# Group 1 of three feed-forward blocks by seven products instead of eight

## The chip, the cores and the metric

The kernel runs on one core of one Trainium2 chip. The metric is device time of one execution in microseconds; the number before the change is the median of three runs, 929.22 us (928.6 to 930.41).

The core's engines that matter: PE (matrix multiply, into eight PSUM banks), DVE (elementwise work), ACT (copies, casts, activation functions), POOL and SP (which here mainly issue transfers from memory). Each engine has its own queue of instructions.

## What is computed

A two-layer encoder trunk on 256 tokens with 1024 channels, in float32. Each layer is

```
x = x + 1/2 * SwiGLU_1(RMSNorm(x))
h = RMSNorm(x);  [qA kA vA qB kB vB] = h @ W_in
x = x + concat(windowed attention A, differential attention B) @ W_out
x = x + 1/2 * SwiGLU_2(RMSNorm(x))
```

with a last RMSNorm, and `swiglu(h) = (silu(h @ w_gate) * (h @ w_up)) @ w_down`. `w_gate` and `w_up` are 1024 x 2816, `w_down` 2816 x 1024. So there are four feed-forward blocks (FFNs), and in this document they are numbered in the order in which they run: 1 and 2 in the first layer, 3 and 4 in the second. The attention parts are not touched by the change.

## The kernel before

**Precision.** Every float32 product is made of three matmuls. An operand is split in a high part (a cast to float32r) and a low part (value minus high part); the product is high·high + low·high + high·low. For the weights the split is done in the kernel: for each half of a weight step, ACT casts (`act.copy(h_, r_)`) and DVE subtracts (`dve.tensor_tensor(l_, r_, f(h_), op=ALU.subtract)`), in `emit_split`. In the profile these are the groups `w<-raw` on ACT and `w<-raw,w` on DVE, 128x1024 each.

**Weight steps.** The list `specs` holds all weight blocks in the order in which PE uses them. A step in an FFN is a block of four 128-row chunks by 512 columns (1 MB). `weights()` takes the next step and calls `ahead(n)`, which writes down loads (`emit_dma`, queue SP), preparations and splits up to half-step n. `look[0]` says how many half-steps the splits run ahead of PE's use: with step i about to be used, half-steps up to 2i + look are written down, and one more when PE reaches the second half of the step (`Split.part`). `IN_FFN` is 8, `IN_MIX` 6.

**Raw buffers.** A loaded block lives in a buffer with the tag `raw`, six of them. The dictionary `raws` keeps the blocks that are still needed; a further load is written down only while it has fewer than `N_RAW = 6` entries. The first two blocks of the kernel are loaded and split by generators (`early`); their entries are removed at the very end of a generator, after its last `yield`.

**An FFN** works on five groups of 512 columns of gate and up (0 to 4), a last part of 256 columns, and the down projection, which runs one group behind. Group 0 needs x as it becomes ready; the inverse norms `r` come from `norm.stats()`, which ends in a small power instruction on POOL. SiLU (ACT) uses r as its scale; the elementwise product `up()` (DVE, two instructions called "ups" below) makes the hidden block h. At the next group PE transposes h (`turn`: four transposes for each of two halves into PSUM, then an ACT cast and a DVE subtraction), and the down projection uses the result. A plain group has 96 matmuls for gate and up and 48 for down.

**Seven products.** Groups in `SEVEN = (2, 3, 4)` do gate and up as a 2 by 2 block product (two token tiles by two halves of the 1024 channels, times two halves of the channels by gate and up) with seven block products of 12 matmuls, `by_seven`. Its weight steps, made by `seven()`, come from four blocks: a (gate, channels 0 to 511), b (up, same), c (up, channels 512 to 1023), d (gate, same). The steps are a; b + c (`bc`); d; c; down0; a + b; that + c; that + d; down1. The sum b + c and the sum a + b are made by transfers from memory on POOL's queue that accumulate into a raw block (`gather`); c and d are added by DVE (`plus`, the group `raw<-raw,raw`). The other side needs four sums of x, made once per FFN by `make_sums()` from float32 copies (`copies()`, eight ACT instructions): each is a DVE subtraction or addition, an ACT cast and a DVE subtraction for its low part. They are made inside group 1, which is plain. The products are combined by seven DVE additions and subtractions (`put`) and two ACT copies.

**Order.** Each engine's instructions keep the order in which the program writes them (`Kept`, `tc.keep_in_program_order`), except inside attention. So the place of a call in the Python text sets what stands behind what on DVE, ACT and POOL. This is the plain group 1 before, with the sums between its parts:

```
tokens(gs, norm.xs, weights(), 0); hT = turn(h, 2); norm.copies()
tokens(gs, norm.xs, weights(), 4); g = gate(gs); next(sums, None)
for k0 in (0, 4): tokens(us, norm.xs, weights(), k0); next(sums, None)
h = hidden(g, us)
for hh in range(2): down(hT, n - 1, hh, weights()); ...
```

Of the kernel before, what the change touches and what calls it, by code (L numbers as in the profile page):

```python
# [12 lines left out]
ALU = mybir.AluOpType  # L13

P = 128
D = 1024
S = 256
# [10 lines left out]
AHEAD = 10  # L28
N_RAW, N_S4 = 6, 28
IN_FFN, IN_MIX = 8, 6  # L30
SEVEN = (2, 3, 4)


@with_exitstack
def trunk(ctx: ExitStack, tc: tile.TileContext, x, n1, g1, u1, d1, nm, w_in, sink,
# [4 lines left out]
    class Kept:  # L40


        def __init__(self, eng):
            self.eng = eng
# [67 lines left out]
        kn = src.shape[1]  # L112
        return Step(kn, n, lambda t: [(t, src)], **how)

    def seven(wg, wu, c0, downs):
# [21 lines left out]
        return [Step(4, 512, load(a), key=a, free=[]),  # L137
                Step(4, 512, load(b), key=b, behind=gather(c, b), prep=gather(b, a)),
                Step(4, 512, load(d), key=d, free=[]),
                Step(4, 512, load(c), key=c, free=[]),  # L140
                downs[0],
                Step(4, 512, None, src=a, free=[]),
                Step(4, 512, None, prep=plus(c, a), src=a, free=[c]),
                Step(4, 512, None, prep=plus(d, a), src=a, free=[a, d]),
                downs[1]]

    def emit_dma(i):
        s = specs[i]
        raws[s.key] = raw = wp.tile([P, s.kn, s.n], F32, tag="raw", bufs=N_RAW, name=nm_("raw"))
        for dst, src in s.moves(raw):  # L150
            if i > 1:
                sp.dma_start(dst, src)
            else:
                for k in range(s.kn):
                    sp.dma_start(dst[:, k:k + 1], src[:, k:k + 1])
                    yield
        if s.behind is not None:
            s.behind()

    class Split:  # L160

# [79 lines left out]
        return w  # L241

    for l in range(DEPTH):
        def ffn_specs(wg, wu, wd):
            down = lambda g, h: plain(wd[l], h * 512, 512, 4 * g, 4)
            for k0 in (0, 4):
                specs.extend(plain(w[l], 0, 512, k0, 4) for w in (wg, wu))
            for g in range(1, NGRP):
                downs = [down(g - 1, h) for h in range(2)]
                if g in SEVEN:  # L250
                    specs.extend(seven(wg[l], wu[l], g * 512, downs))
# [11 lines left out]
        ffn_specs(g1, u1, d1)  # L263
# [21 lines left out]
        ffn_specs(g2, u2, d2)  # L285


    xk = const.tile([P, 2, D], F32, name="xk")

    class Norm:  # L290


        def __init__(self, g0, sums=len(SEVEN) > 0):
# [39 lines left out]
        def make_sums(self):  # L333

            self.sm = []

            (t0, t1), (b0, b1) = [(t[:, :, 0:P], t[:, :, P:S]) for t in self.xg]

            def make(x, y, op):
                v = tmp().rearrange("p a (c s) -> p (a c) s", c=2)  # L340
                dve.tensor_tensor(v, x, y, op=op)
                tag, n = ("q", 3) if len(self.sm) < 3 else ("v", 1)
                sm = tp.tile([P, 2, 512], F32R, tag=tag, bufs=n, name=nm_(tag)).rearrange("p a (c s) -> p (a c) s", c=2)
                act.copy(sm[:, :, 0:P], v)
                dve.tensor_tensor(sm[:, :, P:S], v, f(sm[:, :, 0:P]), op=ALU.subtract)
                self.sm.append(sm)
                return v

            s1 = make(b1, t1, ALU.subtract)
# [18 lines left out]
        def stats(self, n=512):  # L368
# [41 lines left out]
    def take_x(k):  # L410
# [8 lines left out]
        elif k == 1:  # L419
# [6 lines left out]
            norm.pair(3)  # L426
            norm.squares(0, 512, 512)
        elif k == 2:
            ahead(7)
            norm.squares(1, 512, 512)  # L430
            norm.stats()
            constants()
# [131 lines left out]
            elif k == 2:  # L564
                self.nxt.stats()

    def ffn(norm, aside=None, before=None, final=False):
        def silu(out_, acc, t):
            act.activation(out_, acc, AF.Silu, scale=norm.r[:, t:t + 1])
            return out_  # L570
# [25 lines left out]
                pe.matmul(acc, lhsT=xh, rhs=lo, start=False, stop=k == 3)  # L596
            return acc

        def by_seven(h, g):


            flat = lambda: tmp().rearrange("p a n -> p (a n)")
# [3 lines left out]
                return o  # L606

            m1, m7 = flat(), flat()
            act.copy(m1, prod(norm.quarter(0, 0), weights()))
            act.copy(m7, prod(norm.summed(2), weights(held=True)))  # L610
            hT = turn(h, 2)
            p2 = prod(norm.quarter(0, 1), weights())
            g0 = put(flat(), p2, m1, ALU.add)
            p3 = prod(norm.summed(3), weights())
            silu(g0, g0, 0)
            down(hT, g - 1, 0, weights())
            h = blk(F32)
            p5 = prod(norm.summed(0), weights())
            late = g == max(SEVEN)
# [14 lines left out]

        def turn(hs, n):
            out_ = []
            for i in range(n):
                sl = halves(bank())
                for c in range(2):
                    for t in range(2):  # L640
# [12 lines left out]
        gs, us = [bank(), bank()], [bank(), bank()]  # L653
        if before is None:
            before = norm.late
        look[0] = IN_FFN
        before(0)
        ws = (weights(), weights(2))
        for k in (0, 2):
# [2 lines left out]
            for sl, w in zip((gs, us), ws):  # L662
                tokens(sl, norm.xs, w, 0, (k, k + 1))
        before(2)
        tokens(gs, norm.xs, weights(), 4)
        g = gate(gs)
        tokens(us, norm.xs, weights(), 4)
        h = hidden(g, us)
        for n in range(1, NGRP):
            sums = norm.make_sums() if n + 1 == min(SEVEN, default=0) else iter(())  # L670
            if n in SEVEN:
                look[0] = IN_FFN - max(0, n - 2) if before is not take_x else IN_MIX - (n == NGRP - 1)
                h = by_seven(h, n)
                continue
            gs = [bank(), bank()]
            tokens(gs, norm.xs, weights(), 0)
            hT = turn(h, 2)
# [30 lines left out]
    def ffn_end(parts, last):  # L708
# [39 lines left out]
    def mix(l, norm, nxt_norm):  # L748
# [215 lines left out]
        def out_part(w, k0, h, order=None):  # L964
            tokens(accs[h], oT, w, k0, range(2), order=order, h=h)

        for k0 in (0, 2, 4):
            w = weights()
            for h in range(2):
# [25 lines left out]

    for l in range(DEPTH):
        final = l == DEPTH - 1
        parts = ffn(norm, attention_constants, take_x) if l == 0 else ffn(norm)
        norm_m = Norm(16 + l * 8, False)
        ffn_close(parts, norm_m)  # L1000
        norm2 = Norm(32 + l * 8)
# [80 lines left out]
```

## Time and profile before

| | |
|---|---|
| median of three runs | 929.22 us |
| profiled execution, its time | 928.39 us |
| profiled execution, its span | 926.6 us |
| PE busy | 915.1 us |
| DVE busy | 760.8 us |
| ACT busy | 568.7 us |
| bytes read from memory | 192.71 MB |

The profiled execution is 0.8 us below the median, and its span, from the first to the last instruction, 1.8 us below its own time. In the profile nearly every instruction has line L50, that of the wrapper `Kept`, so groups are told apart by what they write and read: `ps<-w,s` is a matmul of x or h with weights, `ps<-w,q` and `ps<-w,v` one with a sum of x, `ps<-ident,s` a transpose of h, `tmp<-ps,tmp` a combination of products. A row of the timeline has start, length, engine, operation, tiles and count; in brackets behind it stands how long the engine was idle before it and what it waited for. A row with a count covers several instructions in a run. [...] FFN 1 runs from 5 to about 188 us, FFN 2 from about 286 to 472, FFN 3 from about 463 to 645, FFN 4 from about 741 to the end.

### The profile page before, as it was taken

How to read it: one execution, taken by the hardware profiler on the slowest of the kernel's cores; microseconds unless marked ns; L12 is line 12 of the kernel's file. 1: busy time of each engine (PE TensorE's matmuls, PEld its weight loads, DVE VectorE, ACT ScalarE, POOL GpSimd, SP SyncE). 2: the span in 40 equal slices, each digit the busy share in tenths (PEclk: the TensorE clock that was granted, in tenths of full speed). 3: DMA queues.
4: the chain of work that ended last, by engine and by line, in shares of the span. 5: the costliest groups of instructions: out<-in, count | busy, mean ns of one | idle time of the engine just before them, and what ended most of it. 6: DMA issues, size and time to landing. Idle time of an engine off the chain costs nothing.

```text
span 926.6 us, 12551 instructions
## 1 busy us (share of the span) xinstructions
PE 915.1 (99%) x4732; PEld 771.7 (83%) x4732; DVE 760.8 (82%) x1074; ACT 568.7 (61%) x893; POOL 59.5 (6%) x77
## 2 busy tenths in 40 slices
PE   8999999999999999999999999999999999999997
PEld 6888887899888888888888888888998888888886
DVE  6759999969876579999776799996698676799994
ACT  7836675557755557576475466565578475566561
POOL 0500000000000001000000000000001000001011
PEclk9999999999999999999999999999999999999999
DMA  9986897827434859797767597887462377597731
GB/s 338 358 224 195 253 279 262 239 98 222 135 124 167 255 152 264 188 261 270 260 234 194 144 298 204 252 279 204 114 226 92 137 231 197 143 292 221 229 118 46
DMA packets 110893, 194.58 MB, mean 210 GB/s; under 512 B 3566, under 2 KB 31280, under 8 KB 110832
## 3 DMA queue, kind: packets, MB, share of 16 engines
q1 hardware_dynamic: 96528, 166.74, 53.1%
q0 software_dynamic: 12928, 25.46, 15.4%
q10 hardware_dynamic: 1376, 1.57, 0.5%
q8 instruction: 37, 0.61, 0.3%
q14 instruction: 24, 0.20, 0.1%
HBM read 192.71 MB, written 1.05 MB: 209 GB/s over the span
## 4 chain that ended last, share of the span: by engine, by line
PE 84%; DVE 9%; issue 2%; DMA 2%; ACT 1%; POOLq 0%; ACTq 0%; POOL 0%; DVEq 0%
PE ps L50 84%; DVE w L50 6%; DMA raw<-in_ffn_w_up_dram 2%; DVE tmp L50 2%; DVE raw L50 1%; ACT w L50 1%; DVE s L50 1%; DMA xk<-in_x_dram 0%; ACT s L50 0%; DVE xk L50 0%; POOLq L1077 0%; ACTq L50 0%; ACT tmp L50 0%; POOL rf L50 0%; DVEq L50 0%
## 5 line engine op out<-in xcount | busy, mean ns | idle before, releaser
L50 PE MATMUL ps<-w,s 128*128 128x512 f32 (+1 forms) x2754 | 640.9, 391 | 0.5 <-DVE w L50 0.5
L50 PEld LDWEIGHTS ps<-w,s 128*128 128x128 f32 x2754 | 512.1, 188 | 106.5 <-DVE w L50 1.2
L50 DVE TENSOR_TENSOR w<-raw,w 128x1024 fp32r<-128x1024 f32 (+1 forms) x440 | 461.1, 1095 | 58.8 <-ACT w L50 57.8
L50 ACT CAST w<-raw 128x1024 fp32r<-128x1024 f32 (+1 forms) x440 | 390.8, 948 | 90.6 <-DVE raw L50 68.1
L50 PE MATMUL ps<-w,q 128*128 128x512 f32 x432 | 101.9, 389 | 0.0
L50 PEld LDWEIGHTS ps<-w,q 128*128 128x128 f32 x432 | 81.1, 188 | 16.8
L50 PE MATMUL ps<-s,w 128*128 128x256 f32 x672 | 84.0, 285 | 0.0
L50 PEld LDWEIGHTS ps<-s,w 128*128 128x128 f32 x672 | 81.7, 192 | 1.1
L50 ACT ACTIVATE s<-ps,gcol 128x256 fp32r<-128x256 f32 (+1 forms) x80 | 31.4, 488 | 44.6 <-PE ps L50 42.9
L50 DVE TENSOR_TENSOR raw<-raw,raw 128x1024 f32<-128x1024 f32 x48 | 56.5, 1218 | 0.0
L50 POOL DMA_DIRECT2D raw<-in_ffn_w_up_dram x24 | 31.1, 1295 | 352.5 <-DVE w L50 166.5
L50 ACT CAST s<-ps 128x512 fp32r<-128x512 f32 x44 | 23.9, 592 | 40.7 <-PE ps L50 40.7
L50 DVE TENSOR_TENSOR s<-ps,s 128x512 fp32r<-128x512 f32 x44 | 28.4, 683 | 19.9 <-ACT s L50 19.9
L50 PE MATMUL ps<-ident,s 128*128 128x128 f32 x304 | 40.5, 274 | 0.6 <-DVE s L50 0.6
L50 PEld LDWEIGHTS ps<-ident,s 128*128 128x128 f32 x304 | 35.0, 140 | 6.9 <-DVE s L50 1.5
L50 ACT ACTIVATE tmp<-tmp,r 128x512 f32<-128x512 f32 x24 | 17.3, 722 | 33.8 <-DVE tmp L50 33.8
L50 ACT ACTIVATE s<-s,negm 128x256 f32<-128x256 f32 x64 | 31.9, 501 | 6.6 <-DVE negm L50 6.4
L50 PE MATMUL ps<-w,v 128*128 128x512 f32 x144 | 34.6, 389 | 0.0
L50 ACT CAST q<-tmp 128x512 fp32r<-128x512 f32 x20 | 12.4, 621 | 35.0 <-DVE tmp L50 34.9
L50 PEld LDWEIGHTS ps<-w,v 128*128 128x128 f32 x144 | 27.0, 188 | 5.6
L50 DVE SCALAR_TENSOR_TENSOR s<-ps,gcol,s 128x256 fp32r<-128x256 f32 x48 | 20.3, 478 | 12.1 <-ACT s L50 12.0
L50 ACT COPY tmp<-ps 128x512 f32<-128x512 f32 x28 | 16.3, 583 | 22.5 <-PE ps L50 22.0
(106 smaller groups left out, 419.5 us busy)
## 6 DMA issues: line engine op xcount, KB each, us to landing
raw<-in_ffn_w_down_dram SPq DMA_DIRECT2D x44, 1024.0 KB, 5.5
raw<-in_ffn_w_gate_dram SPq DMA_DIRECT2D x39, 1024.0 KB, 5.6
raw<-in_ffn_w_up_dram SPq DMA_DIRECT2D x39, 1024.0 KB, 5.3
raw<-in_ffn_w_up_dram POOLq DMA_DIRECT2D x24, 1024.0 KB, 10.4
raw<-in_w_in_dram SPq DMA_DIRECT2D x14, 1024.0 KB, 5.4
raw<-in_ffn_w_gate_dram SPq DMA_DIRECT2D x8, 512.0 KB, 6.4
raw<-in_ffn_w_up_dram SPq DMA_DIRECT2D x8, 512.0 KB, 7.4
raw<-in_w_in_dram SPq DMA_DIRECT2D x8, 512.0 KB, 5.3
```

Of the source, the lines that this page charges most:

```text
L50: ins = issue(*a, **k)
```

## The change

- FFNs 2, 3 and 4 do groups 1 to 4 by seven products; FFN 1 keeps groups 2 to 4.
- In group 1 the steps come in another order: a; d; down0; c; b + c; a + b; + c; + d; down1. So two products with unsummed x and weights and the first half of the down projection stand in front of the products with sums.
- The float32 copies of x and the first two sums move into group 0, the other two into group 1 between its products; the low part of a sum is made one call later than the sum (`low`), and the order of the last two sums is exchanged.
- h is transposed in two halves, one behind each of the first two products.
- In group 0 the splits run 7 half-steps ahead in place of 8; from group 1 to 4 it is 8, 7, 6, 5 (before: 8, 7, 6 from group 2 to 4).
- Accumulating transfers that would be written down while POOL still has to make the next r are kept in a list (`issue`, `hold`) and written right behind it (`flush`).
- The generators of the first two blocks are run to their end, so that their two entries leave `raws`: six blocks instead of four can then be entered. The number of buffers stays six.

```diff
-SEVEN = (2, 3, 4)
+SEVEN = ((2, 3, 4), (1, 2, 3, 4))
...
+        bc = Step(4, 512, load(b), key=b, behind=gather(c, b))
+        rest = [Step(4, 512, load(d), key=d, free=[]), Step(4, 512, load(c), key=c, free=[]), downs[0]]
+        steps = [rest[0], rest[2], rest[1], bc] if first else [bc] + rest
+        steps[0].prep = lambda: issue(gather(b, a))
+        return [Step(4, 512, load(a), key=a, free=[])] + steps + [
                 Step(4, 512, None, src=a, free=[]),
                 Step(4, 512, None, prep=plus(c, a), src=a, free=[c]),
                 Step(4, 512, None, prep=plus(d, a), src=a, free=[a, d]),
...
+    def issue(add):
+        pending.append(add)
+        if not hold[0]:
+            flush()
+
+    def flush():
+        hold[0] = False
+        while pending:
+            pending.pop(0)()
...
             s1 = make(b1, t1, ALU.subtract)
+            s2 = make(s1, t0, ALU.add)
+            low(0, s1)
             yield
-            s2 = make(s1, t0, ALU.add)
+            b0_ = make(b0, s2, ALU.subtract)
+            low(1, s2)
             yield
-            make(t1, t0, ALU.subtract)
+            v = make(t1, t0, ALU.subtract)
+            low(2, b0_)
             yield
-            make(b0, s2, ALU.subtract)
+            low(3, v)
             yield
...
             pool.tensor_tensor(self.r, ms, mhalf[:, 0:2], op=ALU.pow)
+            flush()
...
         elif k == 2:
+            for e in early:
+                next(e, None)
             ahead(7)
...
+                w = weights()
+                next(sums, None)
+                p1 = prod(norm.quarter(0, 0), w)
+                hT = turn(h, (0,))
+                w = weights()
+                next(sums, None)
+                act.copy(m1, p1)
+                p2 = prod(norm.quarter(0, 1), w)
+                hT += turn(h, (1,))
+                w = weights()
+                next(sums, None)
+                g0 = put(flat(), p2, m1, ALU.add)
+                silu(g0, g0, 0)
+                down(hT, 0, 0, w)
+                p3 = prod(norm.summed(2), weights())
+                act.copy(m7, prod(norm.summed(3), weights()))
...
-        look[0] = IN_FFN
+        look[0] = IN_FFN - (1 in sevens)
...
-        tokens(gs, norm.xs, weights(), 4)
+        w = weights()
+        sums = iter(())
+        if 1 in sevens:
+            norm.copies()
+            sums = norm.make_sums()
+        tokens(gs, norm.xs, w, 4)
         g = gate(gs)
-        tokens(us, norm.xs, weights(), 4)
+        w = weights()
+        next(sums, None)
+        tokens(us, norm.xs, w, 4)
         h = hidden(g, us)
...
-                look[0] = IN_FFN - max(0, n - 2) if before is not take_x else IN_MIX - (n == NGRP - 1)
-                h = by_seven(h, n)
+                look[0] = IN_FFN + min(sevens) - n if before is not take_x else IN_MIX - (n == NGRP - 1)
+                h = by_seven(h, n, sums)
...
         look[0] = IN_MIX
+        hold[0] = True
```

More of the change, by code (lines that the diff above doesn't have):

```diff
@@ L113, in plain, with seven @@
         return Step(kn, n, lambda t: [(t, src)], **how)
-    def seven(wg, wu, c0, downs):
+    def seven(wg, wu, c0, downs, first):
         a, b, c, d = [object() for _ in range(4)]
@@ L135, in plus @@
             return prep
[L137 to L141, printed above, removed]
+        bc = Step(4, 512, load(b), key=b, behind=gather(c, b))
[3 more added lines that the diff above has]
+        return [Step(4, 512, load(a), key=a, free=[])] + steps + [
                 Step(4, 512, None, src=a, free=[]),
@@ L157, in emit_dma @@
         if s.behind is not None:
-            s.behind()
+            issue(s.behind)
+    pending, hold = [], [False]
+    def issue(add):
[6 more added lines that the diff above has]
+            pending.pop(0)()
     class Split:
@@ L249, in ffn_specs @@
                 downs = [down(g - 1, h) for h in range(2)]
-                if g in SEVEN:
-                    specs.extend(seven(wg[l], wu[l], g * 512, downs))
+                if g in sevens:
+                    specs.extend(seven(wg[l], wu[l], g * 512, downs, g == 1))
                 else:
@@ L284, in trunk, with __init__ @@
         fine.update(range(mixed + 2, len(specs)))
-        ffn_specs(g2, u2, d2)
+        ffn_specs(g2, u2, d2, SEVEN[1])
     xk = const.tile([P, 2, D], F32, name="xk")
     class Norm:
-        def __init__(self, g0, sums=len(SEVEN) > 0):
+        def __init__(self, g0, sums=True):
             self.g0, self.xs, self.sums = g0, [], sums
@@ L565, in late, with ffn @@
                 self.nxt.stats()
-    def ffn(norm, aside=None, before=None, final=False):
+    def ffn(norm, aside=None, before=None, final=False, sevens=SEVEN[1]):
         def silu(out_, acc, t):
@@ L597, in prod, with by_seven @@
             return acc
-        def by_seven(h, g):
+        def by_seven(h, g, sums):
             flat = lambda: tmp().rearrange("p a n -> p (a n)")
@@ L608, in by_seven @@
             m1, m7 = flat(), flat()
[L609 to L616, printed above, removed]
+            if g > 1:
+                act.copy(m1, prod(norm.quarter(0, 0), weights()))
+                act.copy(m7, prod(norm.summed(3), weights(held=True)))
+                hT = turn(h, 2)
+                p2 = prod(norm.quarter(0, 1), weights())
+                g0 = put(flat(), p2, m1, ALU.add)
+                p3 = prod(norm.summed(2), weights())
+                silu(g0, g0, 0)
+                down(hT, g - 1, 0, weights())
+            else:
+                w = weights()
[9 more added lines that the diff above has]
+                next(sums, None)
+                g0 = put(flat(), p2, m1, ALU.add)
+                silu(g0, g0, 0)
+                down(hT, 0, 0, w)
+                p3 = prod(norm.summed(2), weights())
+                act.copy(m7, prod(norm.summed(3), weights()))
             h = blk(F32)
             p5 = prod(norm.summed(0), weights())
-            late = g == max(SEVEN)
+            late = g == max(sevens)
             p6 = prod(norm.summed(1), weights(look[0] - 5 if late else 0, late))
@@ L636, in turn @@
             out_ = []
-            for i in range(n):
+            for i in (range(n) if isinstance(n, int) else n):
                 sl = halves(bank())
@@ L965, in out_part @@
             tokens(accs[h], oT, w, k0, range(2), order=order, h=h)
+        hold[0] = True
         for k0 in (0, 2, 4):
@@ L997, in trunk @@
         final = l == DEPTH - 1
-        parts = ffn(norm, attention_constants, take_x) if l == 0 else ffn(norm)
+        parts = ffn(norm, attention_constants, take_x, sevens=SEVEN[0]) if l == 0 else ffn(norm)
         norm_m = Norm(16 + l * 8, False)
```

11 lines of the change are left out of this document (6 added, 5 removed).

## The prediction

> **What bounds the kernel now.** I read the page first, then the chain of waits, then the stages of one feed-forward block (FFN), and last its instructions in order of time.
>
> ```profile
> span 926.6 us, 12551 instructions
> PE 915.1 (99%) x4732; PEld 771.7 (83%) x4732; DVE 760.8 (82%) x1074; ACT 568.7 (61%) x893; POOL 59.5 (6%) x77
> PE 84%; DVE 9%; issue 2%; DMA 2%; ACT 1%; POOLq 0%; ACTq 0%; POOL 0%; DVEq 0%
> ...
> 132.63 0.98 PE L50 MATMUL ps<-ident,s 128*128 128x128 f32 x7 [0.34 <-DVE s L50]
> 150.97 13.46 PE L50 MATMUL ps<-w,s 128*128 128x512 f32 x58 [0.54 <-DVE w L50]
> ```
>
> PE works 915.1 of 926.6 us, so a matmul that goes away can shorten the run. But the chain runs through DVE for 9% without PE standing still there: DVE arrives just in time, and in the first FFN twice too late (0.34 and 0.54 us). Which engine would arrive last after the change is read from the stages of the second FFN: group 0's last part, group 1 (plain), groups 2, 3 and 4 (seven products).
>
> ```profile
> 293.40:315.29 21.89, 21.89 (x100) 18.08 (x99) 13.78 (x18) 13.84 (x20) 2.03 (x2) 1.00 0.84 246
> 315.29:346.13 30.84, 30.84 (x142) 25.66 (x141) 21.77 (x24) 19.04 (x28) 1.28 (x1) 1.00 0.57 167
> 346.13:376.94 30.81, 30.81 (x142) 25.61 (x140) 27.76 (x29) 20.02 (x23) 2.57 (x2) 1.00 0.94 263
> 376.94:407.79 30.85, 30.85 (x142) 25.61 (x141) 30.27 (x32) 19.82 (x23) 2.57 (x2) 1.00 0.80 230
> 407.79:437.60 29.81, 29.81 (x137) 24.79 (x136) 29.67 (x33) 19.30 (x24) 0.00 (x0) 1.00 0.79 253
> ```
>
> The columns are length, then busy time of PE, weight loads, DVE, ACT, POOL, then granted clock, DMA share and GB/s. PE is full in all. DVE is idle 8.1 us in group 0's part and 9.1 in group 1, 3.1 in group 2, and 0.6 and 0.1 in groups 3 and 4: groups of seven live on a lead that DVE has won in groups 0 and 1. The change takes group 1's slack.
>
> **The gain.** A plain group has 2 tensors x 2 token tiles x 8 chunks x 3 matmuls = 96 for gate and up, seven products 7 x 4 x 3 = 84: 12 fewer, beside 48 of the down projection.
>
> ```profile
> 293.42 22.03 PE L50 MATMUL ps<-w,s 128*128 128x512 f32 x96
> 315.29 1.04 PE L50 MATMUL ps<-ident,s 128*128 128x128 f32 x8
> 348.85 1.03 PE L50 MATMUL ps<-ident,s 128*128 128x128 f32 x8
> 349.64 2.98 PE L50 MATMUL ps<-w,s 128*128 128x512 f32 x12
> 360.62 5.60 PE L50 MATMUL ps<-w,q 128*128 128x512 f32 x24
> 366.06 11.04 PE L50 MATMUL ps<-w,s 128*128 128x512 f32 x48
> ```
>
> 24 matmuls start 5.44 us before the next row (360.62 to 366.06): 0.227 each; eight transposes take 0.79 (348.85 to 349.64). Twelve are 2.72 us, in three FFNs 8.2 us. With nothing else the profiled 928.39 becomes 920.2.
>
> **What is added.** Each FFN gets six more half-step splits (an ACT cast and a DVE subtraction each), four DVE additions of raw blocks, seven DVE additions of products, two ACT copies and two accumulating transfers on POOL; the sums of x (four additions, casts and subtractions) stay eight DVE instructions but move to an earlier time.
>
> ```profile
> 303.96 1.28 ACT L50 ACT_TABLE_LOAD   x1 [3.02 <-PE ps L50]
> 305.26 1.27 ACT L50 ACTIVATE tmp<-ps,r 128x512 f32<-128x512 f32 x2
> 306.42 3.89 ACT L50 CAST w<-raw 128x1024 fp32r<-128x1024 f32 x4
> 307.50 2.36 DVE L50 TENSOR_TENSOR w<-raw,w 128x1024 fp32r<-128x1024 f32 x2 [3.31 <-ACT w L50]
> 309.77 1.40 DVE L50 SCALAR_TENSOR_TENSOR s<-ps,hr,tmp 128x512 f32<-128x512 f32 x2
> 315.92 1.07 ACT L50 CAST s<-ps 128x512 fp32r<-128x512 f32 x2 [5.62 <-PE ps L50]
> 316.54 1.29 DVE L50 TENSOR_TENSOR s<-ps,s 128x512 fp32r<-128x512 f32 x2 [3.10 <-ACT s L50]
> 316.88 3.04 ACT L50 ACTIVATE s<-ps,gcol 128x256 f32<-128x256 f32 x8
> 320.90 2.36 DVE L50 TENSOR_TENSOR w<-raw,w 128x1024 fp32r<-128x1024 f32 x2 [3.07 <-ACT w L50]
> 323.17 0.68 DVE L50 TENSOR_TENSOR tmp<-s,s 128x512 f32<-128x512 f32 x1
> 323.89 0.62 ACT L50 CAST q<-tmp 128x512 fp32r<-128x512 f32 x1 [0.92 <-DVE tmp L50]
> 324.55 0.69 DVE L50 TENSOR_TENSOR q<-tmp,q 128x512 fp32r<-128x512 f32 x1 [0.69 <-ACT q L50]
> 346.38 0.59 ACT L50 COPY tmp<-ps 128x512 f32<-128x512 f32 x1 [3.29 <-PE ps L50]
> 352.73 2.35 DVE L50 TENSOR_TENSOR raw<-raw,raw 128x1024 f32<-128x1024 f32 x2
> 360.22 9.16 DVE L50 TENSOR_TENSOR w<-raw,w 128x1024 fp32r<-128x1024 f32 x8
> 361.39 8.63 ACT L50 CAST w<-raw 128x1024 fp32r<-128x1024 f32 x9
> 374.63 2.00 DVE L50 TENSOR_TENSOR tmp<-tmp,ps 128x512 f32<-128x512 f32 x3
> ```
>
> Spacings: a split 1.15 us on DVE (9.16/8), a cast 0.96 on ACT (8.63/9), a raw addition 1.15 (2.35/2, following ones closer), a product addition 0.65, a sum, its cast and its low part 0.62 to 0.69 with 0.04 of handover (323.17, 323.89, 324.55), the two products with SiLU ("ups") 1.40. DVE gets 6.9 + 4.6 + 4.6 = 16.1 us more per FFN. Before, the five windows left it 21.0 idle; after them 21.0 - 16.1 - 2.7 = 2.2 would remain, so there is room only if DVE never waits.
>
> It does wait, since engines keep the written order. The row at 320.90 shows it: DVE stood 3.07 us for a cast, although the sum behind it (323.17) had its inputs from 319.92 on, when the eight copies ended (316.88 + 3.04). [...]
>
> So I lay the new order end to end, from 307.50, on the clock of these rows. Splits run one half less ahead in group 0 (seven, not eight), so what DVE does at 307.50 is the second half of down0. Then come two sums (to 309.9), the low part of the first after its cast (to 310.65), and the first half of c, whose cast waits on ACT behind both sum casts (310.5 to 311.55): DVE 311.6 to 312.75. Only then come the ups, 312.75 to 314.15; before they ran at 309.77.
>
> PE needs them for the first transposes. Group 0 ends at 309.8 (ups started at 309.77 when it was done), product 1 takes 2.7, to 312.5. Before, two down halves' worth of slack lay here (transposes at 315.29). Now PE **waits 1.7 us**, to 314.2. Four transposes (0.4), product 2 (2.7) and four transposes bring it to 317.75 and to down0, which needs the cast and split of the first transposed half.
>
> DVE has c's second half and bc's first to 316.45, the sum b0 - s2 to 317.05, a low part to 317.65. ACT has the cast of that sum (317.15), bc's second half (317.65 to 318.7), then the cast of the turned half, to 319.25: PE **waits 1.5**. Its second matmul needs the split, which stands on DVE behind bc's second half (318.75 to 319.9) and ends at 320.6: **waits 1.1**. Eleven matmuls, 2.5 us, to 323.1.
>
> The other turned half: DVE does ab's first half to 321.65, sum and low part to 322.85; ACT the cast of that sum, the copy of product 1 and the cast of ab's second half to 324.3, then the turned cast to 324.95: PE **waits 1.85**. DVE does ab's second half to 325.5, two raw additions to 327.8, and the turned split to 328.5: PE **waits 3.35**.
>
> Sum: 1.7 + 1.5 + 1.1 + 1.85 + 3.35 = 9.5 us lost, 2.7 gained, 6.8 us net per FFN. While PE waited DVE worked on, so groups 2 to 4 begin with DVE further ahead; I take 0 for them. The other two FFNs have the same stages (the windows from their groups 1 on read alike), so 3 x 6.8 = 20.4 us.
>
> **The rest.** The two transfers per FFN are held back behind the POOL instruction that makes r, then issued in turn (about 301.7 and 303).
>
> ```profile
> raw<-in_ffn_w_up_dram POOLq DMA_DIRECT2D x24, 1024.0 KB, 10.4
> ACT w L50 <- DMA raw<-in_ffn_w_up_dram: 16.3, 8, 7.3
> 301.01 0.69 POOL L50 TENSOR_TENSOR r<-ms,mhalf 128x2 f32<-128x2 f32 x1 [38.92 <-DVE ms L50]
> ```
>
> With 10.4 us to landing they are there at 312.1 and 313.4, when ACT wants them at about 312.5 and 319.2: covered. Behind a late one stand bc's casts and with them the turned halves; its price is bounded by 0 and the longest such wait, 7.3 us per FFN; I take 0, nearest to the computed landings. Holding transfers back costs 0, since r is made before they are wanted; were they first in POOL's queue, r and both SiLUs would wait. Six raw buffers for four: in both versions a load at run time waits for one of six buffers, only the count by which loads are written down differed, by two entries never removed. Bounds: a gain of the 0.9 us that PE lost in the first FFN, and a loss of one longest wait, 7.3 us; I take 0, since PE shows no wait for a load of weights that a buffer held up. The first FFN keeps its plain group 1; the sums' low parts, one step later there, lie in slack like that of the second window row, and cost 0.
>
> Profiled run: 928.39 + 20.4 = 948.8; the median, 929.22, is 0.8 higher, so 949.6, **950 us**.
>
> **Rivals.** *DVE keeps up* (faster): the ups and turned splits get done in time, by less work ahead of them or another order than written. Then only the 2.72 us count: 929.2 - 8.2 = 921 us. It decides at 2.72 us of waiting per FFN. Against it: between 307.5 and the last turned split stand 17.5 us of DVE work (seven splits 8.0, two raw additions 2.3, four sums and three low parts 4.5, ups 1.4, turned splits 1.3), and PE wants that split at 318.8, 11.3 us later. 7%.
>
> *No gaps*: DVE and ACT hand over so that DVE does those 17.5 us without a pause, ending at 325.0. PE waits 6.2 us, net 3.5 per FFN: 929.2 + 10.5 = 940 us. For it speaks that I may place single casts too late; against it the rows of 3.31 and 3.07 us in which DVE waits for ACT in just this stage. 15%.
>
> *The clock falls*: the five waits would be by far the longest idle time of PE inside the work.
>
> ```profile
> 907.47 12.75 PE L50 MATMUL ps<-w,s 128*128 128x512 f32 x72
> 923.00:924.00 1.00, 0.00 (x0) 0.00 (x0) 0.00 (x0) 0.00 (x0) 0.00 (x0) 1.00 0.49 186
> 925.00:926.60 1.60, 0.00 (x0) 0.00 (x0) 0.00 (x0) 0.00 (x0) 0.00 (x0) 0.63 0.00 0
> ```
>
> At the end PE stops at 920.2, the clock is still whole at 924 and falls only in the last window, so after some 5 us. If one wait of 3.35 us with its neighbours did the same, the 24 matmuls of down0, 5.4 us, would run at half rate: 5.4 us more per FFN at most, 966 us; I count half of it, 958. [...] 13%. *Late transfers or lost lead* in groups 2 to 4 end in the same place: 1 to 3 us per FFN, 953 to 959. 15%. My own sum (945 to 953): 48%. Unchanged within 0.2% (1.9 us, what a measurement can tell) would need waits of 2.1 to 3.3 us: 2%.
>
> **Numbers.** Faster 0.07, same 0.02, slower 0.91. The range leaves out the faster and unchanged cases (9%) and about half of the clock's: 936 to 960.
>
> **What would show it.** Right: in FFNs 2, 3 and 4 a PE wait of some 2 us before the four transposes of group 1 and further ones inside down0, released by DVE and ACT's turned tiles, 8 to 11 us in all per FFN; groups 2 to 4 as before, 30.8 us each; 36 fewer matmuls. Wrong: PE idle under 3 us there, DVE reaching the ups by 311, or waits on DMA in place of DVE.

## The result and the profile after

The changed kernel takes 967.5 us (median of six runs, 967.25 to 968.75) against 929.43 (928.6 to 930.41) for the kernel before beside it: 1.0411 times the time, 95% interval 1.0398 to 1.0425. Slower was right; 950 us and the range up to 960 were too low. The profiled run spans 965.7 us, 39.1 more than before.

From the page of the kernel after: span, and busy time by engine.

```profile
span 965.7 us, 12600 instructions
...
PE 921.3 (95%) x4696; PEld 771.9 (80%) x4696; DVE 808.3 (84%) x1125; ACT 590.8 (61%) x917; POOL 64.9 (7%) x83
```

PE has its 36 matmuls less (4696 for 4732), yet stands still 44.4 us in place of 11.5. The view of waits, kernel after, PE alone (in all, how often, the longest), names what it waits for:

```profile
PE ps L50 <- DVE s L50: 14.7, 11, 3.1
PE ps L50 <- ACT tmp L50: 13.1, 1, 13.1
PE ps L50 <- ACT s L50: 5.1, 4, 1.5
```

The first and third were forecast: the hidden block h, turned, and its cast and split. The second, one wait of 13.1 us, was not. Matching PE rows of the two timelines place the 39.1 us: one at the start of FFN 2 moves from 293.42 to 307.29, one at the start of FFN 3 from 470.87 to 494.05, of FFN 4 from 747.50 to 777.96, and one late in FFN 4 from 907.47 to 946.60. So FFN 1, whose product order did not change, loses 13.9 us, and FFNs 2, 3 and 4 lose 9.3, 7.3 and 8.7.

**FFN 1.** POOL's timeline of the kernel before, the row in which it makes r:

```profile
27.52 0.72 POOL L50 TENSOR_TENSOR r<-ms,mhalf 128x2 f32<-128x2 f32 x1 [26.02 <-DVE ms L50]
```

The timeline of the kernel after, all engines from 14 to 62 us, that row and those that wait for it:

```profile
41.42 1.48 POOL L50 DMA_DIRECT2D raw<-in_ffn_w_up_dram  x1 [39.91 <-DMA raw<-in_ffn_w_up_dram]
42.43 1.25 POOL L50 TENSOR_TENSOR r<-ms,mhalf 128x2 f32<-128x2 f32 x1
...
43.71 1.27 ACT L50 ACTIVATE tmp<-ps,r 128x512 f32<-128x512 f32 x2 [12.99 <-POOL r L50]
...
44.45 7.14 PE L50 MATMUL ps<-w,s 128*128 128x512 f32 x24 [13.13 <-ACT tmp L50]
```

POOL's queue holds an accumulating transfer ahead of r. It adds into a block that is itself still being loaded, so POOL stands until 41.42; r comes at 43.7 in place of 28.2, the SiLUs behind it, and PE, which waits for the SiLUs, goes on 13.13 us late. The clock, below, adds to that: the 24 matmuls of the row at 44.45 take 6.97 us up to the next row (51.42), and 24 take 5.44 at the full clock.

**Group 1 of FFN 2.** The same five stages as the prediction's windows, with their borders at the same instructions (the last two rows are groups 3 and 4; columns as there):

```profile
307.27:327.59 20.32, 19.32 (x87) 15.72 (x86) 13.11 (x19) 17.99 (x30) 3.35 (x3) 1.00 0.68 148
327.59:369.32 41.73, 36.15 (x140) 28.50 (x141) 37.19 (x41) 22.09 (x26) 2.57 (x2) 0.88 0.80 230
369.32:400.16 30.84, 30.84 (x141) 25.61 (x140) 28.52 (x29) 19.93 (x23) 2.57 (x2) 1.00 0.81 232
400.16:430.98 30.82, 30.82 (x142) 25.61 (x140) 30.71 (x33) 20.13 (x23) 2.57 (x2) 1.00 0.87 254
430.98:460.79 29.81, 29.81 (x137) 24.73 (x136) 29.33 (x32) 18.53 (x23) 0.00 (x0) 1.00 0.79 244
```

The first row has 12 matmuls less than before (product 1's 12 where a plain group does 24 ahead of its transposes) and is 1.57 us shorter, the last three are what they were (30.81, 30.85, 29.81 before). The second is 41.73 in place of 30.84 us, and in it the granted clock is 0.88 on average. The waits in it, from PE's timeline:

```profile
327.59 0.30 PE L50 MATMUL ps<-ident,s 128*128 128x128 f32 x1 [1.00 <-DVE s L50]
...
333.11 0.49 PE L50 MATMUL ps<-w,s 128*128 128x512 f32 x1 [1.21 <-ACT s L50]
334.48 4.81 PE L50 MATMUL ps<-w,s 128*128 128x512 f32 x12 [0.88 <-DVE s L50]
342.43 5.06 PE L50 MATMUL ps<-w,s 128*128 128x512 f32 x11 [3.14 <-DVE s L50]
```

and DVE's rows that end the first and the last of them:

```profile
326.70 1.40 DVE L50 SCALAR_TENSOR_TENSOR s<-ps,hr,tmp 128x512 f32<-128x512 f32 x2
...
338.28 1.23 DVE L50 TENSOR_TENSOR w<-raw,w 128x1024 fp32r<-128x1024 f32 x1 [1.51 <-ACT w L50]
339.42 2.35 DVE L50 TENSOR_TENSOR raw<-raw,raw 128x1024 f32<-128x1024 f32 x2
341.69 0.68 DVE L50 TENSOR_TENSOR s<-ps,s 128x512 fp32r<-128x512 f32 x1
```

Just as in the forecast order, the second turned half (341.69) stands on DVE behind a weight split and two raw additions. A row says more than its bracket: the matmul of 333.11 is alone, and the next starts at 334.48, 1.37 us on and not 0.227. The bracket says 0.88, since a lone matmul's own length (0.49) is taken off; the wait cost 1.14.

**The clock.** Windows of the kernel after at three of its slow stretches; the number behind POOL is the granted clock:

```profile
33.80:47.45 13.65, 3.00 (x7) 2.42 (x8) 3.74 (x5) 3.74 (x5) 5.98 (x9) 0.50 0.64 182
...
334.20:337.60 3.40, 3.12 (x7) 2.48 (x8) 2.56 (x4) 1.41 (x3) 0.00 (x0) 0.50 0.74 251
341.00:347.80 6.80, 5.37 (x13) 4.21 (x14) 5.02 (x7) 2.37 (x3) 0.00 (x0) 0.50 1.01 192
```

So there were three things to take apart: the 13.9 us in FFN 1, the waits, and the halved clock.

### The profile page after: what moved, and what is told of

It reads as the page before. It is cut to its first block, busy times and chain, and to the rows that moved or that the text cites. A ratio compares the mean times of both kernels' runs of the same rounds, so it can differ in the third digit from the quotient of the medians.

```text
span 965.7 us, 12600 instructions
## 1 busy us (share of the span) xinstructions
PE 921.3 (95%) x4696; PEld 771.9 (80%) x4696; DVE 808.3 (84%) x1125; ACT 590.8 (61%) x917; POOL 64.9 (7%) x83
## 3 DMA queue, kind: packets, MB, share of 16 engines
q10 hardware_dynamic: 1376, 1.57, 0.5%
## 4 chain that ended last, share of the span: by engine, by line
PE 83%; DVE 7%; DMA 4%; ACT 3%; issue 1%; POOL 0%; SPq 0%; ACTq 0%; POOLq 0%; DVEq 0%
PE ps L50 83%; DVE w L50 4%; ACT w L50 2%; DMA raw<-in_ffn_w_up_dram 1%; DMA raw<-in_ffn_w_gate_dram 1%; DVE tmp L50 1%; DVE s L50 1%; DVE raw L50 1%; DMA xk<-in_x_dram 1%; ACT tmp L50 1%; ACT L50 0%; ACT q L50 0%; ACT v L50 0%; POOL raw L50 0%; SPq L153 0%
## 5 line engine op out<-in xcount | busy, mean ns | idle before, releaser
L50 PE MATMUL ps<-w,s 128*128 128x512 f32 (+1 forms) x2574 | 614.2, 396 | 30.9 <-ACT tmp L50 13.1
L50 PEld LDWEIGHTS ps<-w,s 128*128 128x128 f32 x2574 | 484.5, 191 | 136.2 <-ACT tmp L50 14.3
L50 DVE TENSOR_TENSOR w<-raw,w 128x1024 fp32r<-128x1024 f32 (+1 forms) x458 | 484.0, 1100 | 56.3 <-ACT w L50 54.3
L50 ACT CAST w<-raw 128x1024 fp32r<-128x1024 f32 (+1 forms) x458 | 409.6, 952 | 102.9 <-DVE raw L50 86.2
L50 PE MATMUL ps<-w,q 128*128 128x512 f32 x540 | 127.7, 390 | 0.0
L50 PEld LDWEIGHTS ps<-w,q 128*128 128x128 f32 x540 | 101.9, 189 | 21.4
L50 DVE TENSOR_TENSOR raw<-raw,raw 128x1024 f32<-128x1024 f32 x60 | 70.6, 1217 | 0.0
L50 POOL DMA_DIRECT2D raw<-in_ffn_w_up_dram x30 | 39.1, 1357 | 409.8 <-DVE w L50 138.2
L50 PE MATMUL ps<-w,v 128*128 128x512 f32 x180 | 43.3, 389 | 0.0
L50 DVE TENSOR_TENSOR tmp<-ps,tmp 128x512 f32<-128x512 f32 x49 | 33.4, 682 | 1.6 <-PE ps L50 1.6
```

What stands on the lines that cost most here:

```text
L50: ins = issue(*a, **k)
```

## Experiments: FFN 1

**The drained generators alone**, in the kernel before.

```diff
             elif k == 2:
+            for e in early:
+                next(e, None)
             ahead(7)
```

> The kernel before, with nothing but the two first generators run to their end (six entries in place of four). Theory A: the accumulating transfer of group 2 gets ahead of r in FFN 1 alone, later FFNs have a wait of the same kind only if their transfer is written before r there too: 929.4 + 13.9 = 943.3 us if FFN 1 alone is hit, up to 929.4 + 4 x 13 = 981 if all four are. Rival C: no change, 929.4.

Measured 943.58 us, 1.016 [1.0139, 1.0181]. Its PE timeline has the same single wait:

```profile
43.63 6.55 PE L50 MATMUL ps<-w,s 128*128 128x512 f32 x17 [12.48 <-ACT tmp L50]
```

Two lines that execute nothing themselves cost 14.9 us. With two more free entries in `raws`, `ahead(7)` writes down a further load and its accumulating transfer, and that comes ahead of `stats()`, which makes r.

**r first.** In the changed kernel, transfers are held from the start on, as they are from FFN 2 on.

```diff
-    pending, hold = [], [False]
+    pending, hold = [], [True]
```

> The changed kernel, but transfers that accumulate are also held back in the first FFN until the POOL instruction that makes r has been written (the flag starts as true). Theory A: the 13.1 us wait of PE in FFN 1 (and the clock at half behind it) comes from one accumulating transfer standing ahead of r in POOL's queue; then r is made at about 27.5 us again, FFN 1 is back to its time before, and the run takes 967.5 - 13.9 = 953.6 us (952 to 955). Rival B: six raw blocks loading at once at the start make all loads late, and PE waits for them whatever POOL's order is; then the time stays at 962 or more.

Measured 951.72 us, 1.0257 [1.0236, 1.0277], a little below what was expected. POOL's timeline of that run:

```profile
26.98 0.72 POOL L50 TENSOR_TENSOR r<-ms,mhalf 128x2 f32<-128x2 f32 x1 [25.48 <-DVE ms L50]
40.78 1.50 POOL L50 DMA_DIRECT2D raw<-in_ffn_w_up_dram  x1 [13.09 <-DMA raw<-in_ffn_w_up_dram]
```

The transfer still waits 13 us for its load, but nothing urgent stands behind it. The order on POOL, not the number of blocks, made the loss in FFN 1: both runs, one from each side, put it near the 13.9 us of the traces (14.9 added to the kernel before, 15.8 taken from the kernel after). Of the 15.8 not all is FFN 1's: the way from the row of matmuls that starts at 14.70 in the kernel after, at 14.09 in this run, to the start of FFN 2 is 14.5 us shorter (292.59, 278.10).

**Without the drained entries**, the rest of the change kept.

```diff
-            for e in early:
-                next(e, None)
```

> The changed kernel without running the two first generators to their end, so that four raw blocks are entered in place of six. Theory A (POOL's order): with four, the load of the block that the transfer adds to is written down only after r, the transfer falls behind r by itself, and FFN 1 loses nothing: about 953.6 us, and up to 3 us per FFN more where group 1 now lacks entries for its blocks (953 to 962). Rival C: the entries have nothing to do with it; 967.5.

Measured 963.63 us, 1.0375 [1.0353, 1.0397], above what was expected. FFN 1 is whole again, but group 1 of FFNs 2 to 4 is worse than in e1_r_first. The timeline of all engines in FFN 2:

```profile
316.24 1.05 ACT L50 CAST w<-raw 128x1024 fp32r<-128x1024 f32 x1 [3.56 <-DMA raw<-in_ffn_w_up_dram]
...
321.28 0.50 PE L50 MATMUL ps<-w,s 128*128 128x512 f32 x1 [3.17 <-ACT s L50]
```

With four blocks entered b + c arrives late, ACT waits 3.56 us for it, and the turned half's cast stands behind (at 320.65). So group 1 by seven does need the six entries; they are harmful only where they let a transfer get in front of r.

**Group 1 plain again**, everything else as in e1_r_first.

```diff
-SEVEN = ((2, 3, 4), (1, 2, 3, 4))
+SEVEN = ((2, 3, 4), (2, 3, 4))
```

> All of the change but its main part: the order of the sums, six entries, transfers held behind r (from the start on), and groups 2 to 4 by seven in all four FFNs; group 1 stays plain. My theory: seven products in group 1 are the whole of what is left, so this takes the time of the kernel before, 929.4 us (within 2). Rival: the parts around it cost or gain something of their own, a difference over 2 us.

Measured 928.08 us, 0.9991 [0.9981, 1.0001]: not to be told from before. What e1_r_first loses beyond that, 23.6 us, belongs to group 1 by seven products.

## Experiments: the waits and the clock

**Fillers.** Matmuls that nobody reads, put where PE waits.

```diff
+        def fill(n):
+            acc, x = bank(), norm.xs[0]
+            for _ in range(n):
+                pe.matmul(acc, lhsT=x[:, 0, 0:P], rhs=x[:, 0], start=True, stop=True)
...
+                fill(4)
                 hT = turn(h, (0,))
...
+                    if t == 0 and k % 2 == 0:
+                        fill(6 if k else 4)
...
+                    pe.matmul(accs[0][t], lhsT=xh, rhs=hi, start=k == 0, stop=False)
+                    if t == 0 and k % 2 == 0:
+                        fill(13 if k else 3)
```

> The kernel of e1_r_first (r first on POOL) with matmuls that nobody reads put into the places of group 1 where TensorE waits: 4 before the first turn, then 4, 3, 6 and 13 between the tokens of the first down stage; they write a spare PSUM bank. In that kernel's trace TensorE is idle there for 1.00, 0.27, 1.20, 0.89, 1.51 and 3.15 us in the second FFN, and half-clock stretches (6.83 us, two of 3.41, 6.83) follow in FFNs two to four; some 6.0 us of them lie under matmuls. Theory A (idle time inside a window is what halves the clock): the granted clock stays full in the three stages, the waits themselves stay, and the time is 951.7 - 6.0 = 945.7 (943 to 948). Theory B (the waits end when DVE and ACT are ready, and the slow matmuls only fill time that would be waited anyway): no change, 950 to 953. If the fillers merely add their 30 x 0.227 us three times, it is up to 972. All that the reference asks for is still computed.

Measured 950.92 us, 1.0243 [1.0226, 1.026]; e1_r_first had 951.72. By the total alone theory B would be right. The stage itself, from the end of group 0 to the first product with a sum, first in e1_r_first:

```profile
311.49:331.97 20.48, 12.47 (x46) 9.11 (x45) 16.15 (x20) 9.06 (x12) 1.28 (x1) 0.83 0.70 177
```

and with fillers:

```profile
314.74:333.21 18.47, 17.38 (x74) 12.65 (x74) 15.57 (x19) 7.67 (x11) 1.28 (x1) 1.00 0.64 167
```

The clock is whole and the stage 2.0 us shorter. From the start of FFN 2's matmuls to FFN 3's it is 185.63 us against 187.11 (295.44 to 481.07, 292.19 to 479.30): 1.5 us, the rest is given back later in the FFN. From FFN 3's to FFN 4's it is 283.50 against 283.53, and from there to the end 184.8 against 186.9. So from FFN 2's start to the end of the span all is 3.55 us shorter (654.0 against 657.5). The total hides that because the profiled run with fillers reached FFN 2 3.25 us later: 1.65 from a later arrival of x, for which PE waits 2.00 us in place of 0.28 (the same row of matmuls starts at 15.74 and at 14.09), the rest in FFN 1, where the edit changes nothing; why is open (from that row to FFN 2 it takes 279.7 us here, 278.1 in e1_r_first and 279.4 in e6_sums_on_pool below).

So time does come back with the clock, in two of three FFNs, and these differences are no scatter: from FFN 2's start to FFN 3's the kernel before, e3_drain_alone and e4_group1_plain all take 178.23 us. FFN 3 stands apart. In e1_r_first PE does not wait there for the first transposes (498.44, 19.14 us behind the FFN's start), so the fillers in front of them only add time (20.05 us behind it with fillers). Up to these 0.91 us are to be put back, so the halved clock costs, by estimate, 3.55 to 4.5 us of the 23 in all, where 6.0 were expected.

**Sums on POOL.** The four sums' additions and low parts leave DVE.

```diff
+            def make(x, y, op):
...
+                pool.tensor_tensor(v, x, y, op=op)
...
+            for sm, v in zip(self.sm, vs):
+                pool.tensor_tensor(sm[:, :, P:S], v, f(sm[:, :, 0:P]), op=ALU.subtract)
...
-            sums = norm.make_sums()
+            sums = norm.make_sums_pool()
+            next(sums)
```

> The kernel of e1_r_first with the four sums of an FFN made on POOL: their four additions and four low parts leave DVE (8 x 0.68 = 5.4 us in each of FFNs two to four), the casts stay on ACT but come after both SiLUs. Theory A (the five waits of group 1 are DVE's queue: sums stand ahead of ups and splits): most of the 8.0 us of idle per FFN goes and the time falls to 929 to 936. Theory B (the waits are the length of the chain up, transpose, cast, split with too few products between its ends; the sums only fill DVE's own idle time): the waits stay within 0.5 us each and the time is 947 to 953.

Measured 945.08 us, 1.0178 [1.016, 1.0197], between the ranges of the two theories. The timeline of all engines in FFN 2:

```profile
304.22 6.86 POOL L50 TENSOR_TENSOR s<-s,s 128x512 f32<-128x512 f32 x3
304.75 2.94 DVE L50 TENSOR_TENSOR w<-raw,w 128x1024 fp32r<-128x1024 f32 x1 [0.83 <-ACT w L50]
...
311.05 1.29 POOL L50 TENSOR_TENSOR s<-s 128x512 f32<-128x512 f32 x1
...
312.37 0.63 ACT L50 CAST v<-s 128x512 fp32r<-128x512 f32 x1 [0.63 <-POOL s L50]
...
313.97 1.92 DVE L50 TENSOR_TENSOR w<-raw,w 128x1024 fp32r<-128x1024 f32 x1 [4.03 <-ACT w L50]
315.81 1.40 DVE L50 SCALAR_TENSOR_TENSOR s<-ps,hr,tmp 128x512 f32<-128x512 f32 x2
...
316.70 0.30 PE L50 MATMUL ps<-ident,s 128*128 128x128 f32 x1 [3.10 <-DVE s L50]
```

The later waits shrank, but the first grew from 1.00 to 3.10 us: the ups now stand behind a weight split whose cast stands on ACT behind casts that wait for POOL. Taking work off DVE helped less than it should, because POOL was late in another queue, and because DVE itself got slower beside it: the split at 304.75 took 2.94 us and not 1.22, and a POOL addition 6.86/3 = 2.29, though one that ran without DVE's splits beside it (311.05) took 1.29.

So DVE and POOL both got slower side by side; why they did, and what makes up the 2.94 us, no run shows.

**Another order**, sums on DVE and all made ahead of p1: p1, p2, both turns, p3, down0, p7, with loads to match. The look-ahead changes with it: 9 half-steps in place of 7 in group 0, and 7, 6, 5, 4 in place of 8, 7, 6, 5 from group 1 on.

```diff
-        steps = [rest[0], rest[2], rest[1], bc] if first else [bc] + rest
+        steps = rest[:2] + [downs[0], bc] if first else [bc] + rest
...
-                hT = turn(h, (0,))
...
-                hT += turn(h, (1,))
+                hT = turn(h, 2)
+                p3 = prod(norm.summed(2), weights())
...
-                down(hT, 0, 0, w)
-                p3 = prod(norm.summed(2), weights())
+                down(hT, 0, 0, weights())
```

> The order of e7_pool_reorder with the sums left on DVE, all made ahead of p1. If the order alone ends the waits: within 3 us of e7_pool_reorder. If DVE cannot make sums, splits and turns in time: the waits come back ahead of p3 or of the first down stage, 3 to 6 us per FFN, 935 to 950.

The same order with sums on POOL:

> The kernel of e6_sums_on_pool, and group 1 in the order of the other groups as far as its loads allow: p1 and p2, then both turns, then p3, then the first down stage, then p7, with the loads in that order and two steps of look more. Theory B (distance decides): one or two products, 2.7 us each, stand between a result and its use, so of the 8.0 us some 1 to 2 stay per FFN, no window is halved, and the 12 matmuls saved per FFN (2.7 us) come out at last: 922 to 930. Theory A (DVE's queue): as e6_sums_on_pool, or no further gain than 2 us.

Measured 936.32 us for e9_reorder (1.0081 [1.0066, 1.0096]) and 934.71 for e7_pool_reorder (1.0069 [1.0054, 1.0084]). So the order with its look-ahead takes 15.4 of the 23 us back, and the sums' place is worth only 1.6 on top: the two runs lie within 3 us of each other, as was expected if the order decides. This points to distance as the main cause of group 1's waits: the order tried by the change puts the turn one product behind the ups and the first half of down right behind the turn. It is not shown apart from the look-ahead, since no run changes one without the other. Both are still slower than before, though, and e7_pool_reorder's 922 to 930 missed.

What is left is in later groups too. PE's timeline of e9_reorder in FFN 2, group 1 first:

```profile
318.40 0.51 PE L50 MATMUL ps<-w,s 128*128 128x512 f32 x1
319.78 5.51 PE L50 MATMUL ps<-w,s 128*128 128x512 f32 x23 [0.87 <-DVE s L50]
...
347.75 0.98 PE L50 MATMUL ps<-ident,s 128*128 128x128 f32 x7 [0.33 <-DVE s L50]
...
397.08 10.74 PE L50 MATMUL ps<-w,s 128*128 128x512 f32 x46 [0.46 <-DVE w L50]
```

and its windows of groups 2 to 4 (PE, weight loads, DVE, ACT, POOL):

```profile
345.00:376.00 31.00, 30.62 (x139) 25.03 (x138) 30.90 (x33) 19.95 (x24) 2.57 (x2) 1.00 0.84 252
376.00:407.00 31.00, 30.51 (x138) 24.74 (x137) 29.88 (x31) 18.79 (x22) 2.57 (x2) 1.00 0.88 242
407.00:437.00 30.00, 28.95 (x128) 22.79 (x127) 29.89 (x32) 19.18 (x23) 0.00 (x0) 1.00 0.84 253
```

DVE works 30.90 of 31, 29.88 of 31 and 29.89 of 30 us. That suggested that DVE is the bound once PE is no longer held up in group 1. It is no proof: in groups 3 and 4 of the kernel before DVE is as full (30.27 of 30.85, 29.67 of 29.81), and PE loses nothing there.

## Experiments: is DVE the bound then?

**Half of the raw additions on POOL**, in e9_reorder, in e7_pool_reorder, and in e4_group1_plain as the control:

```diff
-                    dve.tensor_tensor(t_, t_, x_, op=ALU.add)
+                    (pool if h else dve).tensor_tensor(t_, t_, x_, op=ALU.add)
```

> The kernel of e9_reorder with the second half of each addition to a raw block (128x1024, 1.17 us on DVE, two halves of it per group by seven) on POOL. In e9_reorder DVE is busy 30.90, 29.88 and 29.89 us of the 31, 31 and 30 us stretches of groups two to four, and TensorE waits there for splits, 0.19 to 0.53 us at a time. Theory C (with group 1 by seven DVE is the bound: 15.5 us more work per FFN and no spare time left in the stage): 2.35 us per group of relief end the waits of groups two to four, and the time falls by 3 to 8 us to 928 to 933; without any wait it would be 928.6 - 3 x 2.7 = 920.5. Rival: POOL takes twice as long for a half (2 x 1.29 = 2.6 us, worked out from its 128x512 operations) and waits for transfers in its queue, so that the summed blocks come late: 937 to 950.

> The kernel of e7_pool_reorder (sums on POOL as well) with the same halves on POOL. Theory C: another 5.4 us off DVE in each of three FFNs, 922 to 931 and not above e10_adds_on_pool. Rival: POOL's queue, now with sums, halves and transfers, is late in group 1: 937 or more.

> The kernel of e4_group1_plain (groups 2 to 4 alone by seven, 928.1) with the same halves on POOL: what the edit does where DVE is not the bound. Theory C: nothing to gain, 926 to 929. Rival: POOL late, 930 to 940; then a loss in e10_adds_on_pool is POOL's and says nothing on DVE.

Measured 997.63 us (1.0738 [1.0722, 1.0754]), 993.39 (1.069 [1.0666, 1.0714]) and 956.89 (1.0305 [1.0285, 1.0324]). The first and the last lie above even the times that the rivals named. The control loses 28.1 us by itself, so, as its expectation said, these runs say nothing on DVE. The groups by costs of e10_adds_on_pool:

```profile
L50 POOL TENSOR_TENSOR raw<-raw,raw 128x1024 f32<-128x1024 f32 x30 | 94.7, 3157 | 106.7 <-DVE w L50 106.7
...
L50 DVE TENSOR_TENSOR w<-raw,w 128x1024 fp32r<-128x1024 f32 x354 | 445.8, 1299 | 106.9 <-ACT w L50 106.0
```

A half takes 3.16 us on POOL (2.6 was expected, 1.22 it takes on DVE), the splits on DVE rise from 1.22 to 1.30 on average, and DVE waits 106.0 us for casts; in e9_reorder that was 43.3.

**Half of the raw additions left out**, in e9_reorder: the summed weights then lack half of c and of d.

```diff
-                for h in (0, 2):
+                for h in (0,):
```

> The kernel of e9_reorder without the second half of each addition to a raw block, and without anything in its place: two operations of 1.17 us per group by seven leave DVE, and part of the summed weights is wrong, so the values differ from the reference. POOL is as in e9_reorder. Theory C (DVE is the bound once group 1 goes by seven): the waits of 0.19 to 0.53 us in groups two to four of FFNs two to four go with the 2.35 us of relief per group, as does the 0.87 of group 1: 926 to 932. Rival (chains of latency with too few products between their ends, whatever DVE has to do): 935 to 937.

Measured 932.52 us, 1.0044 [1.0029, 1.0059]: 3.8 us less than e9_reorder. Its windows of groups 2 to 4:

```profile
345.00:376.00 31.00, 30.66 (x140) 25.17 (x139) 29.06 (x31) 20.13 (x24) 2.57 (x2) 1.00 0.83 242
376.00:407.00 31.00, 30.59 (x139) 25.07 (x138) 28.32 (x30) 19.41 (x24) 2.57 (x2) 1.00 0.95 276
407.00:437.00 30.00, 29.44 (x132) 23.56 (x132) 27.66 (x31) 18.93 (x24) 0.00 (x0) 1.00 0.80 243
```

DVE works 29.06, 28.32 and 27.66 us there, PE's waits for splits fall from 3.9 us in all (ten) to 2.0 (four), and the time falls to just above theory C's range (926 to 932). But waits of 0.88 in group 1 and 0.53 in group 4, which that theory wanted gone, stay in each of FFNs 2 to 4, so DVE's load is a part of the rest and not all of it. No version tried beats the kernel before.

## Why the prediction was wrong, step by step

**The step that failed** is the one on the raw buffers and the first FFN: "Six raw buffers for four: ... I take 0", with "The first FFN keeps its plain group 1", which gave FFN 1 no loss at all. It asked whether a load would wait for a buffer, and bounded the loss by 7.3 us, the longest wait for a transfer seen. The entries act otherwise: they decide how many loads and transfers are written down ahead of r on POOL. The prediction named the mechanism ("were they first in POOL's queue, r and both SiLUs would wait") and dismissed it, since transfers are held back; but `hold` begins as False and becomes True only at the end of an FFN or of an attention part, so the first FFN has no such guard. The term was put at 0 and measured 13.9 us in the trace, 14.9 alone (e3_drain_alone), 15.8 when taken away (e1_r_first).

**The waits of group 1: right, with some luck in the total.** With that repaired the kernel takes 951.7 us against 950 forecast. The stretches that begin with FFNs 2, 3 and 4 are 8.88, 6.89 and 8.56 us longer than before, 24.3 in place of 20.4; less the clock's 3.55 to 4.5 that is 19.8 to 20.8, so the waits were sized well. The total comes nearer to 950 than 24.3 would because that run reached FFN 2 1.2 us earlier than the kernel before (292.19, 293.42), which no step forecast. The last two waits read start to start in e1_r_first are 318.00 to 319.38 and 323.69 to 327.33, less 0.227: 1.15 and 3.41 us, forecast 1.1 and 3.35. The other three show 1.00 with 0.27 behind it, 1.20 and 1.51 in their brackets, which are up to 0.27 short; forecast 1.7, 1.5 and 1.85. That is FFN 2, and FFN 4 reads alike; in FFN 3 the first wait, forecast for all three, is missing. The ups were to start 2.95 us after group 0's end (312.75, 309.8); they start at 326.70, and the row of 84 matmuls that ends at 326.6 has product 1's 12, 2.7 us, at its end: 2.8. The first wait is shorter than laid out because the first transpose goes after the first of the two ups.

**Gain, transfers and later groups: right.** 36 matmuls less, 12 in the row ahead of the first transposes in each FFN (84 for 96); groups 2 to 4 as before. The transfers were taken to cost 0: in group 1 of FFN 2 of e1_r_first no cast of ACT waits for one.

**The clock: a rival that came true.** It was given 13%, 5.4 us per FFN at most and 2.7 counted. The clock did halve in FFNs 2 to 4, and costs an estimated 3.55 to 4.5 us in all three together, 1.5 us of it in FFN 2 (e5_fillers). The half rate in its 5.4 us shows in the kernel before only at the end (granted clock 0.50 from 925.6 us on), in the kernel after inside the work too (0.50, the windows above); that a wait of 3.35 us with its neighbours would bring it, and the 13%, were the author's estimates. In e1_r_first the clock halved at 324.90, when PE had stood still for 0.7 us, behind 3.41 us with 1.18 us of busy PE, below.

**DVE keeps up, no gaps: fell**, as the waits show. The prediction's "2.2 us would remain" idle on DVE was the better warning: with the waits mended by another order, e9_reorder is bound there in part and still 7.7 us slower than before.

## What to carry to other kernels

In a kernel with written order, a limit that only counts (entries, steps of look-ahead) is a change of order: before raising it, list what can now be issued earlier, on every queue, and what urgent small instruction stands behind it, in the first stage too. A saving on the busiest engine is worth nothing if it is paid on the next one: here 2.7 us of PE cost 15.8 us of DVE work per FFN (808.3 less 760.8, in three) in stages that had 21 to spare, and a better order, with its look-ahead, gave back two thirds of what was left of the loss once r came first, but not a gain. Read waits from start to start, and judge the clock by how much of a window PE was idle, not by the longest wait: in the kernel after it halved behind stretches of 3.41 us in which PE was busy 0.38 to 1.62 us.

## What the runs showed of the hardware

**The clock halved behind a window that was partly busy.** e1_r_first, four windows in a row, cut where the clock changes:

```profile
318.08:321.49 3.41, 2.52 (x10) 1.87 (x11) 3.41 (x5) 1.21 (x2) 0.00 (x0) 1.00 0.44 120
321.49:324.90 3.41, 1.18 (x5) 0.41 (x3) 1.90 (x3) 2.14 (x4) 0.65 (x1) 1.00 0.49 188
324.90:328.31 3.41, 0.98 (x2) 0.83 (x3) 3.41 (x4) 1.04 (x1) 0.64 (x1) 0.50 0.61 92
328.31:331.72 3.41, 3.41 (x9) 2.63 (x8) 1.63 (x4) 1.66 (x2) 0.00 (x0) 0.50 1.12 222
```

PE was busy 2.52 us in the first and the clock stayed; 1.18 in the second, in two pieces, and the clock halved for the next; it came back only after the fully busy fourth. When it halved, at 324.90, PE had stood still for 0.7 us (since 323.69 + 0.49).

In the kernel after, the six halved stretches inside the work start at 33.80, 334.18, 341.00, 521.91, 528.74 and 812.04 us and are 13.65, 3.41, 6.83, 3.41, 3.41 and 6.83 us long. In the 3.41 us just ahead of each, at the full clock, PE was busy 0.92, 1.62, 1.61, 1.59, 0.38 and 0.61 us; in the last 3.41 us of each, 3.01, 3.11, 3.41, 3.29, 3.38 and 3.42. PE busy for 1.99 us (341.00 to 344.42) and for 1.56 (812.04 to 815.45) did not bring the full clock back.

**DVE and POOL were slower side by side**, in FFN 2 of e6_sums_on_pool: a split on DVE took 2.94 us in place of 1.22, an addition on POOL 2.29 in place of 1.29.
